# Four conditioning units of a hybrid layer moved from a feed-forward loop to the gaps between attention heads

## The chip, the cores and the metric

The kernel runs on one core of one Trainium2 chip. The metric is the device time of one execution in microseconds (us), as the median of several executions. A profile comes from one further execution, taken by the hardware profiler; its time is given beside the median below.

## What is computed

One layer of a streaming encoder for two requests that share the weights: 1024 prompt frames, and 32 frames of a running stream with caches and states. D is 1024. Cut to what matters here:

```python
mod = jax.nn.silu(c) @ w_ada + b_ada                       # c: one vector per request
sh1, sc1, g1, sh2, sc2, g2 = jnp.split(mod[:, None, :], 6, axis=-1)
h = x * (1 + sc1) + sh1
mq, mk, mv, mo, mi, mf, fq, fk, fv, ff, gu, gv = jnp.split(h @ w_in, split_at, axis=-1)
...                                                        # mLSTM (4 heads), FoX attention (8 heads), gMLP gate
mix = jnp.concatenate([hm, hf, hg], axis=-1) @ w_o
x = _layer_norm(ALPHA * x + (1 + g1) * mix, ln1_g, ln1_b)
h = x * (1 + sc2) + sh2
y = (jax.nn.silu(h @ w_gate) * (h @ w_up)) @ w_down
x = _layer_norm(ALPHA * x + (1 + g2) * y, ln2_g, ln2_b)
```

The first lines are adaLN: six vectors of 1024 values for each request, made from the conditioning vector c. The last of them, `g2`, is used only where the result of the feed-forward's down projection is added to the residual.

## The kernel before, in words

**Numbers and groups.** The 1056 frames stand on the free axis in two groups: group 0 has 512 columns, group 1 has 544. Every large product is done in float32r as three matmuls, with weights and operand each split in a high and a low part (`gemm`, L111 to L119: high by high L117, high by low L118, low by high L119). A weight block of 512 KB is loaded into the ring `raw` (3 buffers of pool `wp`), cast by ScalarE to `whi` (L105), and VectorE makes `wlo` (L106). All loads (L87) and stores (L91) that are spoken of here go through SyncE's queue (SP), one after another.

**The adaLN units.** `mod` is made in 24 units of 256 columns (`ada`, L171 to L189). A unit loads two halves of 512 KB of `w_ada`, does 16 matmuls of 32 x 256 (L179) into one PSUM bank, in four strips of the array, copies the result with ScalarE (L182, `adas`), transposes it with two matmuls into the other half of the same bank (L185), and VectorE reduces it (L187, `adam`) and writes the columns of `mod` (`ada_end`, L191). Units 0 to 7 (`sh1`, `sc1`) are done in the first product. Twelve units, 16 to 19 (`g1`) and 8 to 15 (`sh2`, `sc2`), are done in phase one by `more(n)` (L1344): their weights go to the two buffers `late` of pool `pl`, so a unit takes both, and their bank is one of the two of pool `pt` (tag `t`). Units 20 to 23 (`g2`) are done in the feed-forward of group 0.

**Phase one (up to about 360 us of the span).** A list written out by hand, `ORDER` (L42), says in which order the head projections (`q`, `k`), the first half of the FoX heads (`f`), the mLSTM chunks (`m`), the token-major projections (`v`, `o`) and single adaLN units (`a`) are emitted. PSUM has the ring `g` of three banks (pool `pg`) for the large products, two banks `t`, two `s`, and one `o`.

**Between the phases (to about 475 us).** The columns of the mixers' results for group 0 are read back from a DRAM tile `dmix` (`wo_mix`, loads named `mlstm_al`), group 0's residual is loaded (`wo_z<-xT`, eight loads, L978), the gMLP part runs (`evac_gv`, `evac_gmlp`, with ScalarE's copy `tm_gms`, L703, and its store to `dmix`), and the last projections of the heads' queries and keys (`fm_unit` with `evac_qk`, L359 to L367), then the output projection of group 0 and its layer norm (`ln1`, L1025 to L1042).

**Group 0's feed-forward (to about 886 us).** The rest of the mixers (`mixers`, L1272: second half of the FoX heads, five mLSTM chunks, the sample's attention `foxs`) is emitted first, then the loop over the groups of feed-forward columns (`GROUPS`, L33). `up` (L1072) makes gate and up products in the ring `g` (the program's name is `up_g`), reads them with ScalarE and VectorE (L1090 to L1096), and `down` accumulates groups of three or four columns into the residual. Inside the first columns stands the loop body with `if j < 4`: after each of columns 0 to 3, one adaLN unit 20 + j whose weights go to the ring `raw` and whose bank is one of the three of ring `g`.

At the sixth group (`g == WOB`) the mixers' pools are closed, and group 1's output projection (`wo(1)`) follows: its operand comes from `dmix` through `wo_tmp` loads into pool `pb`, with the casts L975 and L976 (`wo_mix`, L960), and its residual by eight `wo_z` loads. The rest is group 1's feed-forward and the two last layer norms.

**What sets the order.** The program is written in an order, but the Tile scheduler (`schedule_with_timeline_sim=True`) decides in which order each engine's instructions are issued. The order is fixed when the kernel is built; on the chip every engine works its list off in order and waits where an operand or a buffer isn't ready. So a change in one place can move rows elsewhere.

Of the kernel before, what the change touches and what calls it, by code (L numbers as in the profile page):

```python
# [38 lines left out]
MLB = (1, 2, 3, 4, 5)  # L39
RESE = "pp"  # L40
TAFF = ("aaaaaaaa", "aaaaaaav")
ORDER = "k0 k1p q0 f0 q1 a f1 s a q2 f2 a q3 f3 a v q4 f4 a q5 f5 o a m0 q6 f6 a m1 q7 m2 f7 a m3"  # L42
ADAPOS = 4
GENG = (0, 1, 1, 0)
FP = (0, 0)
RAW = 3
# [10 lines left out]
def weave(*parts):  # L57

    parts = list(parts)
    while parts:  # L60
        for p in list(parts):
            if next(p, parts) is parts:
                parts.remove(p)
# [6 lines left out]
class Kernel:  # L70
# [1215 lines left out]
    def run(self):  # L1286
# [52 lines left out]
        sl = ExitStack()  # L1339
        self.pl = self.pada = self.pool("pl", ctx=sl)  # L1340
        w1 = d["w_in_v"]
        rest = list(range(16, 20)) + list(range(8, 16))

        def more(n):  # L1344
            for u in rest[:n]:
# [34 lines left out]

        for x in ORDER.split():
            if x[0] in "fm" and HPA:
# [51 lines left out]
        for g, (j0, nj) in enumerate(GROUPS):  # L1434
            if g == WOB:
                s4.close()
                s3.close()
                self.pu, self.utag = self.pool("pu", 3, space=PSUM), "gu"
                pb = self.pb = self.pool("pb", side="right")
                weave(self.up(0, j0 + 1, act, pa, MM[0]))  # L1440
                self.operand(1, pb)
                with tc.issue_after(self.lastz.ins):
                    self.wo_mix(1, self.KORDER)
                stb = self.ln_begin(nc.gpsimd)
                self.wo(1, stb, MM[1], nc.vector, pb)
                self.operand(1, pb)

                def norm():
                    for a, b in MM[1]:
                        yield from self.ln1(1, stb, a, b)  # L1450

                self.sums()

                def fill():
                    for j in range(j0 + 2, j0 + nj):
                        self.sums()
                        yield from self.up(0, j, act, pa, MM[0])

                weave(fill(), norm())
                continue  # L1460
            for j in range(j0 + (g > 0), j0 + nj + (g < last)):
                weave(self.up(0, j, act, pa, WIDE if 0 < j < GROUPS[-1][0] else MM[0]))
                if j < 4:
                    self.ada(20 + j, self.wp, "raw", RAW, self.pg, "g")
            if g == WOB - 1:
                st = self.ln_begin(nc.gpsimd, sum=False)
                self.down(0, g, act, WIDE, st)
            else:
                self.down(0, g, act, WIDE)
# [160 lines left out]
```

## Time and profile before

| what | value |
|---|---|
| median of 3 runs | 1384.97 us (1381.76 to 1388.18) |
| profiled execution, its own time | 1386.62 us |
| its span | 1384.6 us |
| mean granted TensorE clock | 0.99 |
| TensorE (PE) busy | 1343.1 us, 97% |
| VectorE (DVE) busy | 1031.2 us, 74% |
| ScalarE (ACT) busy | 655.5 us, 47% |
| GpSimd (POOL) busy | 244.8 us, 18% |

The span is the time from the first to the last instruction that the profiler recorded; the profiled execution took 2 us more than that and lies 1.65 us above the median. "Granted clock" is the share of its full speed at which TensorE was clocked. Rows of the timeline give the start, the duration, the engine, the line and the tiles of an instruction, and in brackets how long its engine stood idle before it and whose end it waited for. A number such as x16 is a run of equal instructions; the duration is then that of the run. SPq is the queue in which SyncE issues DMAs: its durations are those of the issue, not of the transfer.

### The profile page before, as it was taken

To read this page: it belongs to the slowest core of one execution; us is meant where nothing else is said; L and a number is where in the kernel's file an instruction comes from. 1 tells how busy PE (TensorE), PEld (TensorE's weight loads), DVE (VectorE), ACT (ScalarE), POOL (GpSimd) and SP (SyncE) were. 2 spreads that over 40 slices of the span, in tenths; PEclk is the share of its full clock that TensorE was granted. 3 is DMA by queue.
4 is the path that set the end of the run, shared out by engine and by line. 5 is a ranking of instruction groups with operands and counts; after the bars stand their busy time and mean duration, and the time that the engine had idled before them with its cause. 6 is when DMAs were issued, how large, how long until landed. Compare 5 with 4: busy or idle time off the path is not lost.

```text
span 1384.6 us, 25402 instructions
## 1 busy us (share of the span) xinstructions
PE 1343.1 (97%) x9459; PEld 1226.1 (89%) x9459; DVE 1031.2 (74%) x2190; ACT 655.5 (47%) x1281; POOL 244.8 (18%) x276
## 2 busy tenths in 40 slices
PE   7999999999999899999999999999999999999996
PEld 4799788989899778888887889899999999999996
DVE  5547774678778757777776766678898988888777
ACT  3313354554545544545544455335564454545355
POOL 0102100042157500000000000264610000000341
PEclk9999999999999999999999999999999999999998
DMA  9763475455764765544444343564596768453321
GB/s 359 248 222 103 138 238 165 133 166 155 251 194 145 204 197 154 142 140 120 135 120 95 108 119 94 189 175 130 157 241 183 211 161 218 133 175 116 101 90 65
DMA packets 126386, 224.67 MB, mean 162 GB/s; under 512 B 21284, under 2 KB 70060, under 8 KB 126264
## 3 DMA queue, kind: packets, MB, share of 16 engines
q1 hardware_dynamic: 120952, 212.95, 49.4%
q0 software_dynamic: 5168, 9.96, 4.8%
q8 instruction: 75, 1.23, 0.4%
q14 instruction: 47, 0.39, 0.1%
q10 hardware_dynamic: 144, 0.14, 0.0%
HBM read 191.21 MB, written 51.72 MB: 175 GB/s over the span
## 4 chain that ended last, share of the span: by engine, by line
PE 83%; DVE 9%; DMA 4%; ACT 2%; issue 2%; POOL 1%; SPq 0%; DVEq 0%; ACTq 0%; POOLq 0%
PE up_g L117 5%; PE up_g L118 5%; PE up_g L119 5%; PE dn_g L119 4%; PE dn_g L117 4%; PE dn_g L118 4%; PE tm_g L282 3%; PE tm_g L283 3%; PE tm_g L284 3%; PE sup_u L119 3%; PE sup_u L117 3%; PE sup_u L118 3%; PE wo_g L118 2%; PE wo_g L119 2%; PE wo_g L117 2%; PE fox_t L788 2%
## 5 line engine op out<-in xcount | busy, mean ns | idle before, releaser
L117 PE MATMUL up_g<-mlstm_ah,up_whi 128*128 128x512 f32 (+1 forms) x384 | 141.3, 368 | 4.2 <-ACT lna_tmp L1037 3.4
L118 PE MATMUL up_g<-mlstm_al,up_whi 128*128 128x512 f32 (+1 forms) x384 | 141.5, 369 | 0.6 <-DVE mlstm_al L1042 0.6
L119 PE MATMUL up_g<-mlstm_ah,up_wlo 128*128 128x512 f32 (+1 forms) x384 | 140.7, 367 | 0.0
L283 PE MATMUL tm_g<-tm_wlo,start_h1h 128*128 128x256 f32 (+1 forms) x384 | 109.8, 287 | 0.0
L282 PE MATMUL tm_g<-tm_whi,start_h1h 128*128 128x256 f32 (+1 forms) x384 | 109.3, 287 | 0.0
L284 PE MATMUL tm_g<-tm_whi,start_h1l 128*128 128x256 f32 (+1 forms) x384 | 108.8, 285 | 0.0
L1161 ACT CAST sup_whi<-sup_raw 128x1024 fp32r<-128x1024 f32 x54 | 56.0, 1047 | 90.8 <-PE dn_u L118 47.4
L117 PEld LDWEIGHTS up_g<-mlstm_ah,up_whi 128*128 128x128 f32 x384 | 73.2, 191 | 16.9 <-ACT mlstm_ah L1041 3.6
L761 ACT ACTIVATE fox_p<-fox_s,fox_fmx 128x384 f32<-128x384 f32 (+2 forms) x96 | 55.2, 578 | 60.6 <-DVE fox_fmx L759 44.3
L118 PEld LDWEIGHTS up_g<-mlstm_al,up_whi 128*128 128x128 f32 x384 | 73.1, 190 | 11.9 <-DVE mlstm_al L1042 1.2
L119 PEld LDWEIGHTS up_g<-mlstm_ah,up_wlo 128*128 128x128 f32 x384 | 73.2, 191 | 10.6
L105 ACT CAST up_whi<-up_raw 128x1024 fp32r<-128x1024 f32 x50 | 52.4, 1048 | 61.6 <-PE up_g L118 18.2
L106 DVE TENSOR_TENSOR up_wlo<-up_raw,up_whi 128x1024 fp32r<-128x1024 f32 x50 | 66.8, 1336 | 14.0 <-ACT up_whi L105 13.3
L1016 DVE SCALAR_TENSOR_TENSOR wo_z<-dn_g,start_mod,wo_z 128x512 f32<-128x512 f32 (+4 forms) x120 | 60.2, 520 | 21.5 <-PE dn_g L119 19.6
L1162 DVE TENSOR_TENSOR sup_wlo<-sup_raw,sup_whi 128x1024 fp32r<-128x1024 f32 x54 | 68.1, 1264 | 10.5 <-ACT sup_whi L1161 10.5
L283 PEld LDWEIGHTS tm_g<-tm_wlo,start_h1h 128*128 128x128 f32 x384 | 72.3, 188 | 2.3 <-issue 2.1
L282 PEld LDWEIGHTS tm_g<-tm_whi,start_h1h 128*128 128x128 f32 x384 | 72.1, 189 | 1.7 <-issue 0.8
L117 PE MATMUL dn_g<-up_acth,dn_whi 128*128 128x512 f32 (+2 forms) x200 | 73.5, 368 | 0.0
L118 PE MATMUL dn_g<-up_actl,dn_whi 128*128 128x512 f32 (+2 forms) x200 | 73.4, 368 | 0.0
L119 PE MATMUL dn_g<-up_acth,dn_wlo 128*128 128x512 f32 (+2 forms) x200 | 73.3, 366 | 0.0
L284 PEld LDWEIGHTS tm_g<-tm_whi,start_h1l 128*128 128x128 f32 x384 | 72.2, 188 | 0.1
L117 PE MATMUL fm_g<-start_h1h,fm_whi 128*128 128x272 f32 (+2 forms) x200 | 60.6, 312 | 5.9 <-DVE fm_qkl L367 2.0
(628 smaller groups left out, 4628.9 us busy)
## 6 DMA issues: line engine op xcount, KB each, us to landing
up_raw<-w_gu SPq DMA_DIRECT2D x50, 512.0 KB
dn_raw<-w_dn SPq DMA_DIRECT2D x28, 512.0 KB
ada_late<-w_ada SPq DMA_DIRECT2D x24, 512.0 KB
wo_raw<-w_o SPq DMA_DIRECT2D x24, 512.0 KB
sup_raw<-w_gu SPq DMA_DIRECT2D x20, 512.0 KB
start_dp<-w_gu SPq DMA_DIRECT2D x19, 512.0 KB
start_dp<-w_gu POOLq DMA_DIRECT2D x19, 512.0 KB, 7.8
sup_raw<-start_dp SPq DMA_DIRECT2D x18, 512.0 KB
```

Source lines behind the costliest of these rows:

```text
L105: nc.scalar.copy(hi[:, :w], raw[:, :w])
L106: (eng or nc.vector).tensor_tensor(lo[:, :w], raw[:, :w], f(hi[:, :w]), ALU.subtract)
L117: nc.tensor.matmul(ps, hi, xh(k), start=start and k == 0, stop=False)
L118: nc.tensor.matmul(ps, hi, xl(k), start=False, stop=False)
L119: nc.tensor.matmul(ps, lo, xh(k), start=False, stop=stop and k == n - 1)
L282: nc.tensor.matmul(ps[:, :ncol], xh, hi, start=k == 0, stop=False)
L283: nc.tensor.matmul(ps[:, :ncol], xh, lo, start=False, stop=False)
L284: nc.tensor.matmul(ps[:, :ncol], xl, hi, start=False, stop=k == 7)
L761: nc.scalar.activation(pr[:, lo:hi], banks[x][:, :hi - lo], AF.Exp, bias=mxs[:, 0:1], accum_out=sums[:, x:x + 1])
L1016: self.lastz = self.nc.vector.scalar_tensor_tensor(z[:, m, x:y], ps[:, x - a:y - a], g[i], z[:, m, x:y], ALU.mult, ALU.add)
L1161: nc.scalar.copy(h, x)
L1162: tt(l, x, f(h), ALU.subtract)
```

## The change

Units 20 to 23 are appended to the list of the units of phase one, `ORDER` gets four more `a`, and the two lines in group 0's feed-forward loop are gone. So these units use the buffers `late` and a bank `t` instead of `raw` and a bank `g`. The number of instructions of every engine and their shapes stay the same.

```diff
-ORDER = "k0 k1p q0 f0 q1 a f1 s a q2 f2 a q3 f3 a v q4 f4 a q5 f5 o a m0 q6 f6 a m1 q7 m2 f7 a m3"
+ORDER = "k0 k1p q0 f0 q1 a f1 s a q2 f2 a q3 f3 a v a q4 f4 a q5 f5 a o a m0 q6 f6 a m1 a q7 m2 f7 a a m3"
...
-        rest = list(range(16, 20)) + list(range(8, 16))
+        rest = list(range(16, 20)) + list(range(8, 16)) + list(range(20, 24))
...
             for j in range(j0 + (g > 0), j0 + nj + (g < last)):
                 weave(self.up(0, j, act, pa, WIDE if 0 < j < GROUPS[-1][0] else MM[0]))
-                if j < 4:
-                    self.ada(20 + j, self.wp, "raw", RAW, self.pg, "g")
```

The scheduler's order differs at three places of interest.

First, SP's queue at the end of phase one. `wo_raw`, `dvn` and `traw` are weights and tiles of the gMLP part, `dmix_32` and `dmix_33` the mixers' results of groups 0 and 1, `mlstm_al` the operand of group 0's output projection, `wo_z` its residual. Before:

```order
L87 DMA wo_raw_4952<-w_o 128x1024
L91 DMA start_dvn_63<-tm_traw_4548 128x256
L87 DMA wo_raw_4989<-w_o 128x1024
L91 DMA start_dvn_63<-tm_traw_4585 32x256
L91 DMA o_vn<-tm_traw_4585 32x256
L87 DMA tm_gvn_4726<-start_dvn_63 128x512
L91 DMA start_dmix_32_88<-fox_fo_3904 64x512
L91 DMA start_dmix_32_88<-mlstm_mixs_4006 128x2x128
L87 DMA mlstm_al_4021<-start_dmix_32_88 128x512 x6
L87 DMA wo_z_787_4040<-xT 128x512 x8
L91 DMA start_dmix_33_89<-tm_gms_4670 128x2x256
```

The same stretch of the changed kernel:

```order
L91 DMA start_dvn_63<-tm_traw_4636 128x256
L87 DMA ada_late_3996<-w_ada 128x1024
L87 DMA ada_late_4002<-w_ada 128x1024
L91 DMA start_dvn_63<-tm_traw_4673 32x256
L91 DMA o_vn<-tm_traw_4673 32x256
L87 DMA tm_gvn_4814<-start_dvn_63 128x512
L91 DMA start_dmix_32_88<-fox_fo_3969 64x512
L91 DMA start_dmix_33_89<-tm_gms_4758 128x2x256
L91 DMA start_dmix_32_88<-mlstm_mixs_4094 128x2x128
L87 DMA tm_gvn_4854<-start_dvn_63 32x256
L87 DMA mlstm_al_4109<-start_dmix_32_88 128x512 x6
L87 DMA wo_z_807_4128<-xT 128x512 x8
```

The two loads of the last adaLN unit stand in the queue here, and the store of `tm_gms` for group 1, which stood behind the eight `wo_z` loads, now stands ahead of them and of the `mlstm_al` loads.

Second, TensorE's list at the start of group 0's feed-forward, where the first column's last gate and up matmuls stand (`up_g` with three different numbers: three banks of ring `g`). Before:

```order
L119 MATMUL up_g_8087<-mlstm_ah_4020,up_wlo_8001 128x256
L117 MATMUL up_g_8062<-mlstm_ah_4020,up_whi_7994 128x256
L117 MATMUL up_g_8087<-mlstm_ah_4020,up_whi_8000 128x256
L179 MATMUL ada_g_8119<-ada_raw_8120,start_c_63_182 32x256 x4
L179 MATMUL ada_g_8119<-ada_raw_8126,start_c_63_182 32x256 x4
L118 MATMUL up_g_8062<-mlstm_al_4021,up_whi_7994 128x256
```

The changed kernel at the same place:

```order
L119 MATMUL up_g_8175<-mlstm_ah_4108,up_wlo_8089 128x256
L117 MATMUL up_g_8150<-mlstm_ah_4108,up_whi_8082 128x256
L117 MATMUL up_g_8175<-mlstm_ah_4108,up_whi_8088 128x256
L117 MATMUL up_g_8221<-mlstm_ah_4108,up_whi_8211 128x512
L118 MATMUL up_g_8221<-mlstm_al_4109,up_whi_8211 128x512
L119 MATMUL up_g_8221<-mlstm_ah_4108,up_wlo_8212 128x512
```

Where the adaLN unit took the next bank of ring `g`, the second column's gate product takes it now.

Third, TensorE's list at the end of group 0's feed-forward: `fox_o` is the output of the last FoX head, `dn_g` a block of 128 rows of the down projection (eight blocks of 12 matmuls in this group, here the third), `dn_t` the sum for the layer norm's pivot. Before:

```order
L801 MATMUL fox_o_7931<-fox_pth_7975,fox_v_7806 128x256
L796 MATMUL fox_o_7931<-fox_ptl_7976,fox_v_7806 64x256
L801 MATMUL fox_o_7931<-fox_pth_7975,fox_v_7806 128x256
L894 MATMUL dn_t_10079<-wo_z_787_4040,start_ones_45_140 128x512
L118 MATMUL dn_g_10104<-up_actl_9856,dn_whi_10100 128x512
L119 MATMUL dn_g_10104<-up_acth_9855,dn_wlo_10101 128x512
```

The changed kernel, at the end of the last of the eight blocks (`dn_g_10191`):

```order
L796 MATMUL fox_o_8019<-fox_ptl_8064,fox_v_7894 64x256
L801 MATMUL fox_o_8019<-fox_pth_8063,fox_v_7894 128x256
L894 MATMUL dn_t_10079<-wo_z_807_4128,start_ones_45_140 128x512
L118 MATMUL dn_g_10191<-up_actl_9712,dn_whi_10172 128x512
L119 MATMUL dn_g_10191<-up_acth_9711,dn_wlo_10173 128x512
L117 MATMUL dn_g_10191<-up_acth_9783,dn_whi_10172 128x512
L118 MATMUL dn_g_10191<-up_actl_9784,dn_whi_10172 128x512
```

Before, 62 matmuls of `dn_g` stood between the last FoX head and the `up` products that lead to group 1's output projection; now there are 8. The 96 `up` matmuls (128x256) behind them are the same in both.

## The prediction

> **What bounds the kernel now.** I read the page first: the busy times of the engines and the chain of waits.
>
> ```profile
> PE 1343.1 (97%) x9459; PEld 1226.1 (89%) x9459; DVE 1031.2 (74%) x2190; ACT 655.5 (47%) x1281; POOL 244.8 (18%) x276
> PE 83%; DVE 9%; DMA 4%; ACT 2%; issue 2%; POOL 1%; SPq 0%; DVEq 0%; ACTq 0%; POOLq 0%
> ```
>
> TensorE bounds the kernel: 97% of 1384.6 us, and 83% of the chain that ended last. It idles for 41.5 us in all. A change that leaves TensorE's work as it is can win only part of those, or of the time at a lower clock, and can lose by adding to either. The busy times by stretch show where they lie (columns: PE, PEld, DVE, ACT, POOL, then granted clock, DMA share, GB/s).
>
> ```profile
> 110.00:180.00 70.00, 66.66 (x452) 59.83 (x451) 52.28 (x144) 25.61 (x60) 12.25 (x22) 0.95 0.45 137
> 250.00:320.00 70.00, 67.13 (x512) 60.47 (x511) 49.39 (x140) 32.63 (x77) 15.22 (x16) 1.00 0.55 169
> 365.00:420.00 55.00, 53.02 (x424) 52.24 (x423) 40.24 (x56) 26.87 (x42) 25.65 (x26) 0.97 0.73 226
> 440.00:475.00 35.00, 28.84 (x221) 27.23 (x220) 28.85 (x62) 21.10 (x49) 26.60 (x33) 0.95 0.54 152
> 475.00:540.00 65.00, 64.67 (x402) 50.48 (x401) 38.48 (x97) 31.78 (x71) 0.74 (x1) 0.97 0.70 199
> 540.00:900.00 360.00, 357.86 (x1908) 301.93 (x1907) 261.92 (x537) 172.91 (x345) 15.53 (x19) 1.00 0.44 126
> ```
>
> Phase one has idle time, 3.34 us in 110 to 180 and 2.87 us in 250 to 320. Group 0's feed-forward, which the units leave, has nearly none: 0.33 us in 475 to 540 and 2.14 us in the 360 us behind. So there is no gap that the units' going closes, and what decides is how the waits at three or four places move.
>
> **The change part by part.**
>
> *A. The moved work.* The timeline shows one unit at each place, its 16 matmuls and its two transposes with the row behind them.
>
> ```profile
> 256.47 1.07 PE L179 MATMUL ada_t<-ada_late,start_c 128*32 128x256 f32 x16
> 261.35 0.38 PE L185 MATMUL ada_t<-start_ident,ada_adas 128*128 128x128 f32 x2
> 261.49 0.36 PE L284 MATMUL tm_g<-tm_whi,start_h1l 128*128 128x256 f32 x1
> ...
> 491.16 1.07 PE L179 MATMUL ada_g<-ada_raw,start_c 128*32 128x256 f32 x16
> 492.16 0.50 PE L117 MATMUL up_g<-mlstm_ah,up_whi 128*128 128x512 f32 x1
> 492.50 0.40 PE L118 MATMUL up_g<-mlstm_al,up_whi 128*128 128x512 f32 x1
> 492.73 0.40 PE L119 MATMUL up_g<-mlstm_ah,up_wlo 128*128 128x512 f32 x1
> ```
>
> The matmuls take 1.07 us in both places; the next row starts 1.00 us after them and 0.14 us after the transposes. With 0.1 us for each of two changes of tile (the row behind takes 0.50 instead of the 0.40 of the two behind it) a unit costs 1.35 us of TensorE. Four leave the feed-forward (-5.4) and four enter phase one (+5.4): 0. The eight loads of 512 KB change queue places but not number.
>
> *B. The banks of the feed-forward.* The tiles `ada_g` borrowed a bank of ring `g` between the gate and up products. Two rows show a wait at such a place.
>
> ```profile
> 473.55 1.07 PE L179 MATMUL ada_g<-ada_raw,start_c 128*32 128x256 f32 x16 [1.69 <-DVE up_sil L1093]
> 478.41 0.50 PE L117 MATMUL up_g<-mlstm_ah,up_whi 128*128 128x512 f32 x1 [0.34 <-DVE ada_adam L187]
> ```
>
> The second wait, for the reduction of the unit, goes: -0.34. The first is a wait for a bank that VectorE was still reading (`up_sil`). In the changed order the second column's gate product (`up_g_8221`) stands where the unit stood and needs the same bank, so the wait stays; only if VectorE has read the bank sooner does it go as well. Bounds -2.0 (0.34 and 1.69) and 0; I take -0.3, since the bank's reader is unchanged.
>
> *C. The clock in the feed-forward.* Three stretches of a few us around the third unit:
>
> ```profile
> 502.00:506.00 4.00, 4.00 (x33) 3.26 (x32) 2.53 (x5) 1.69 (x3) 0.00 (x0) 1.00 0.11 44
> 508.00:511.50 3.50, 3.50 (x36) 2.40 (x35) 1.54 (x4) 1.52 (x5) 0.00 (x0) 1.00 0.63 195
> 511.50:515.00 3.50, 3.50 (x15) 1.94 (x15) 2.42 (x3) 1.37 (x4) 0.00 (x0) 0.53 0.84 232
> ```
>
> TensorE has no idle time in any of them, yet from 511.5 to 515 the granted clock is 0.53, behind a stretch of 32-row adaLN matmuls and small matmuls of the sample's attention. At 0.53 the 3.5 us do what 1.9 us would do: 1.6 us lost. The stretch from 502 to 506, with the sample's matmuls but without a unit, kept 1.00. With the units gone the drop may go (-1.6) or not (0). I take -1.2, three quarters of it, since the row with small matmuls alone kept its clock.
>
> [...]
>
> *D. The transition from phase one.* Here stands the wait that the changed SP order touches.
>
> ```profile
> 362.64 5.97 SPq L87 DMA_DIRECT2D wo_z<-xT  x8
> 369.34 0.38 SPq L91 DMA_DIRECT2D start_dmix<-tm_gms  x1
> ...
> 374.91 0.59 ACT L703 COPY tm_gms<-tm_g 128x512 f32<-128x512 f32 x1 [4.96 <-DMA start_dmix<-tm_gms]
> ...
> 371.39 0.39 PE L117 MATMUL fm_g<-start_h1h,fm_whi 128*128 128x272 f32 x1 [1.98 <-DVE fm_qkl L367]
> ...
> 372.00:374.00 2.00, 2.00 (x10) 2.00 (x10) 0.00 (x0) 0.00 (x0) 0.18 (x1) 0.50 1.06 373
> 374.00:376.00 2.00, 2.00 (x13) 1.97 (x12) 0.00 (x0) 1.09 (x2) 0.00 (x0) 0.71 0.98 317
> ```
>
> The store of `tm_gms` stands in SP's queue behind eight residual loads, and its data moves while the DMA engines are full (share 1.06). ScalarE waits 4.96 us for that store, since its tile has one buffer, and the `g` banks that it reads are held: TensorE waits 1.98 us, and then runs at 0.50 and 0.71 for 4 us, which costs 1.0 and 0.6 us. Together 3.6 us. In the changed order the store stands ahead of the eight loads. But the queue then carries two adaLN loads just ahead, and an instruction that waits there holds the whole queue. Bounds: -3.6 (all gone) and +2 (another wait of 1.98 us in its place). I take -2, a little over half of the gain, since the store is moved but the eight loads still fill the engines right behind it.
>
> *E. New loads in phase one.* Twelve units stand there now.
>
> ```profile
> L179 PE MATMUL ada_t<-ada_late,start_c x192: 379/379/636, 66.2 to 355.6; 128*32 128x256 f32 x192
>   DMA ada_late<-w_ada: 2.8, 1
> ...
> 156.63 0.83 SPq L87 DMA_DIRECT2D ada_late<-w_ada  x2
> 160.97 1.08 PE L179 MATMUL ada_t<-ada_late,start_c 128*32 128x256 f32 x8 [2.81 <-DMA ada_late<-w_ada]
> ...
> 160.00:165.00 5.00, 4.03 (x21) 3.25 (x22) 2.27 (x8) 3.12 (x9) 0.54 (x1) 0.51 0.88 294
> ```
>
> One unit of twelve waited for its loads: issued at 156.63, used at 160.97, 4.3 us later, with 2.81 us of idle time and then a clock of 0.51 for some 4 us (2 us more). A unit occupies both `late` buffers, so its loads can't be issued before the last unit's matmuls, and a second unit close behind the first (the `a a` after `f7`) has to bridge those 4.3 us with other work; in the changed list 34 rows of TensorE stand between. As often as before, four units give 4/12 of 2.81: +0.9. Bounds 0 (each load hidden like eleven of twelve) and +4.8 (one such wait with its clock).
>
> *F. The last FoX head and group 1's output projection.* The mixers' chain of waits isn't shortened by the change, but it starts 5.4 us later and the feed-forward beside it has 5.4 us less to do; in the changed order the last head ends in the last down block.
>
> ```profile
> 870.82 1.02 PE L894 MATMUL dn_t<-wo_z,start_ones 128*128 128x512 f32 x2
> 871.87 0.45 SPq L91 DMA_DIRECT2D start_dmix<-fox_fo  x1
> 874.16 0.33 SPq L87 DMA_DIRECT2D wo_tmp<-start_dmix  x1
> 874.58 3.23 SPq L87 DMA_DIRECT2D wo_z<-xT  x7
> ...
> 887.44 2.73 SPq L87 DMA_DIRECT2D wo_tmp<-start_dmix  x4
> 897.70 0.29 PE L117 MATMUL wo_g<-up_ah,wo_whi 128*128 128x272 f32 x1
> 897.83 0.29 PE L118 MATMUL wo_g<-up_al,wo_whi 128*128 128x272 f32 x1
> 901.15 0.43 DVE L976 TENSOR_TENSOR up_al<-wo_tmp,up_ah 128x272 fp32r<-128x272 f32 x1
> ```
>
> From the head's end at 870.82 to the output projection at 897.70 lie 26.9 us. Now 54 fewer `dn_g` matmuls stand there (62 before, 8 after), each of 512 columns like the rows under A, which follow one another every 0.23 us (492.50 to 492.73): 12.4 us, so about 14.5 us are left. The chain needs 3.3 us to the first load (870.82 to 874.16) and, once the loads flow, 14.1 us to the last cast (887.44 to 901.58): 17.4. TensorE asks for the last operand only at the end of the first block row of `wo_g`, 48 matmuls of 0.13 us (897.70 to 897.83) or 6.2 us after its start: 20.7. A slack of 3.3 us, then. But the eight `wo_z` loads, 8 x 278 KB = 2.2 MB or 6.0 us at 373 GB/s, seven of which were issued from 874.58 on and had the time to themselves, now fall between the operands. Bounds: 0, and +5 (6.0 less 3.3 is 2.7 of idle time, and about 2 of lower clock as in D and E). I take +1.5, nearer to 0, as the changed order puts only four of the loads ahead of most of the operands.
>
> *Sum.* 0 - 0.3 - 1.2 - 2.0 + 0.9 + 1.5 = -1.1 us against the profiled execution's 1386.62: 1385.5. The median of the runs is 1.65 us lower than that execution, so on that scale 1383.9, in round numbers **1384.0**. Half a per cent, about what a measurement of this kernel can tell from no change, is 6.9 us: below 1378.0 and above 1391.9.
>
> **The rivals.**
>
> *Faster: the freed ring.* Here the units' place in the ring was what cost: B goes whole (-2.0), C whole (-1.6), D whole (-3.6), E and F are hidden. That is -7.2 against 1384.97: 1377.8. For it speaks that each of these waits stands in a row above; against it that B's wait has an unchanged reader, and that three things must go right at once, with nothing late next.
>
> *Slower: the mixers' chain becomes the bound ahead of `wo(1)`.* TensorE has no more work to put beside the last head, and waits for store, load and cast. It decides as soon as the operand loads are delayed by more than the slack of 3.3 us. The eight residual loads (6.0 us) and three `w_o` blocks of 512 KB (4.2 us at 373 GB/s) in front of all operands would make 10.2 - 3.3 = 6.9 us idle, and 2 us of lower clock: +8.9; with B, C and E as forecast (-0.6), and D at 0, +8.3 against 1384.97: 1393.3. For it: the 62 matmuls have become 8, and a program whose filler shrinks while its chain does not must wait somewhere. Against it: not all loads stand in front, and 54 matmuls of `dn_g` are cover that the last head now had for itself.
>
> *No effect because nothing moves.* The rows of the order show the units in their new place and TensorE's list changed, so this has no chance worth a number; a total of zero by cancelling is my forecast's own case.
>
> **How the numbers follow.** The forecast gets 0.62: with any one term at either of its ends and the others as taken, the sum lies between -2.8 (B) and +2.9 (D), far within half a per cent. The freed ring gets 0.16, as it needs all of B to D; the chain ahead of `wo(1)` 0.22, as one cause alone decides it and E may add to it. For the range I take 1376.0 (the freed ring, and most of phase one's one wait of 2.81 us gone as well) to 1394.0 (the chain's case); outside is left about one in ten on each side. The chances of faster and slower by over 0.5% are those of the rivals, which end just beyond the bounds: 0.15 and 0.22, with 0.63 within.
>
> **What would show each step right or wrong.** A: the L179 rows of tile `ada_late` become x256, and the time from 475 to 870 falls by 5.4 us while phase one grows by as much. B: no wait for `ada_adam`, and still one of 1 to 2 us for `up_sil` at the first column's end. C: a clock of 1.00 through the sample's attention. D: the store of `tm_gms` lands before the `wo_z` loads are issued, ScalarE's wait of 4.96 us is gone, and the clock from the transition on is 1.00. E: the waits for `ada_late` stay at one, or come at the two units behind the last head. F: between the last `fox_o` and the first `wo_g`, no idle time and a full clock. The prediction is wrong if TensorE's idle time ahead of `wo(1)` exceeds 5 us, if a queue held by an adaLN load delays weights of phase one by more than 5 us, or if the stretches without any such wait differ by more than 1 us from before, for which I have no cause.

## The result, and the profile after

The changed kernel takes 1397.06 us (median of 5 runs, 1392.75 to 1398.19), the kernel before 1386.75 us (5 runs). The ratio is 1.007 with a 95% interval of 1.0055 to 1.0086: slower by about 10 us, outside the forecast's range. The profiled execution took 1397.91 us, with a span of 1395.9 us against 1384.6.

The page of the changed kernel, busy times and chain of waits:

```profile
PE 1344.2 (96%) x9459; PEld 1226.7 (88%) x9459; DVE 1034.1 (74%) x2190; ACT 656.2 (47%) x1281; POOL 249.7 (18%) x276
PE 77%; DVE 10%; DMA 7%; ACT 2%; issue 2%; POOL 1%; SPq 1%; DVEq 0%; ACTq 0%; POOLq 0%
```

TensorE is busy for as long as before (1344.2 against 1343.1 us). Nearly all of the added time is idle time: 51.7 us now, 41.5 before. In the chain, DMA has risen from 4% to 7%. Where the time lies is seen by the same landmarks in both traces:

| landmark on TensorE | before | after | difference so far |
|---|---|---|---|
| first matmul behind the layer norm's wait (`up_g`, wait for `lna_tmp`) | 466.16 | 471.18 | +5.0 |
| first matmul of group 1's output projection (`wo_g`) | 897.70 | 905.37 | +7.7 |
| the wait for `up_wlo` behind it | 1010.31 | 1021.28 | +11.0 |
| end of the span | 1384.6 | 1395.9 | +11.3 |

The first 5.0 us are in the main the four units' own work, now ahead of the first landmark (0.86 us of it is the layer norm's wait, 4.24 us where it was 3.38). Behind it the units' 5.4 us should have been won back. Instead another 2.7 us were lost up to `wo_g` (so 8 us of new loss there), and 3.3 us at its start. The busy times by stretch of the changed kernel:

```profile
365.00:420.00 55.00, 52.58 (x432) 51.47 (x431) 40.34 (x62) 27.38 (x44) 23.41 (x22) 1.00 0.76 240
475.00:540.00 65.00, 56.16 (x311) 45.71 (x311) 35.42 (x76) 27.40 (x62) 3.55 (x8) 0.92 0.50 130
...
485.00:495.00 10.00, 2.88 (x13) 2.09 (x12) 6.61 (x12) 7.39 (x13) 0.73 (x1) 0.88 0.41 118
495.00:505.00 10.00, 10.00 (x62) 7.59 (x62) 2.96 (x6) 1.99 (x3) 0.00 (x0) 0.78 0.29 89
```

From 475 to 540 TensorE was busy for 64.67 us before; now it is 56.16, at a clock of 0.92. Between 485 and 495 it works for 2.88 us of 10. The waits are in the timeline of TensorE:

```profile
478.56 0.50 PE L117 MATMUL up_g<-mlstm_ah,up_whi 128*128 128x512 f32 x1 [1.72 <-DVE up_sil L1093]
...
494.57 0.80 PE L117 MATMUL up_g<-mlstm_ah,up_whi 128*128 128x512 f32 x1 [7.12 <-DVE up_sil L1092]
495.17 0.63 PE L118 MATMUL up_g<-mlstm_al,up_whi 128*128 128x512 f32 x1
...
910.84 0.52 PE L117 MATMUL wo_g<-up_ah,wo_whi 128*128 128x272 f32 x2 [2.30 <-ACT up_ah L975]
```

The first wait, 1.72 us, is the one that the forecast expected to stay (1.69 before). The second, 7.12 us, is new: the up product of the second column needs a bank of ring `g`, and VectorE has not read the first column's gate product (L1092). Behind it the granted clock is 0.50 from 494.57 to 499.46, which costs 2.4 us more (a matmul takes 0.63 instead of 0.40 us). The third, 2.30 us, is new too.

Why the bank was read so late is seen on the engines that read it. ScalarE and then VectorE of the changed kernel:

```profile
486.12 0.42 ACT L576 ACTIVATE mlstm_mo<-mlstm_mo 128x256 f32<-128x256 f32 x1 [7.18 <-DMA mlstm_mo<-start_dmo]
...
487.92 0.38 ACT L1089 ACTIVATE up_sil<-up_g 128x256 f32<-128x256 f32 x1
...
489.85 0.63 ACT L587 ACTIVATE mlstm_mw<-mlstm_mw 128x512 f32<-128x512 f32 x1 [0.32 <-DVE mlstm_mw L585]
...
492.21 0.41 ACT L1091 ACTIVATE up_sil<-up_sil 128x256 f32<-128x256 f32 x1
```

```profile
488.20 1.62 DVE L585 SCALAR_TENSOR_TENSOR mlstm_mw<-mlstm_mb,start_col,start_maskbig 128x128 f32<-128x128 f32 x4 [3.68 <-DMA mlstm_mb<-start_dM]
...
490.11 1.23 DVE L106 TENSOR_TENSOR up_wlo<-up_raw,up_whi 128x1024 fp32r<-128x1024 f32 x1
...
491.70 2.36 DVE L106 TENSOR_TENSOR up_wlo<-up_raw,up_whi 128x1024 fp32r<-128x1024 f32 x2
494.10 0.42 DVE L1092 TENSOR_TENSOR up_sil<-up_g,up_sil 128x256 f32<-128x256 f32 x1
```

ScalarE waits 7.18 us for a load of the first mLSTM chunk (`mlstm_mo`), and the first exponential of the gate product (L1089) stands behind that wait. VectorE waits 3.68 us for another load of the chunk (`mlstm_mb`); behind it come four mLSTM instructions and three weight splits (L106), and only then the read of the bank. The same rows of the kernel before, ScalarE, then VectorE and the first matmul of the second column's up product on TensorE:

```profile
478.37 0.38 ACT L1089 ACTIVATE up_sil<-up_g 128x256 f32<-128x256 f32 x1
481.39 0.42 ACT L576 ACTIVATE mlstm_mo<-mlstm_mo 128x256 f32<-128x256 f32 x1 [2.64 <-DMA mlstm_mo<-start_dmo]
```

```profile
482.21 1.14 DVE L585 SCALAR_TENSOR_TENSOR mlstm_mw<-mlstm_mb,start_col,start_maskbig 128x128 f32<-128x128 f32 x4 [2.25 <-DMA mlstm_mb<-start_dM]
483.27 0.41 DVE L1092 TENSOR_TENSOR up_sil<-up_g,up_sil 128x256 f32<-128x256 f32 x1
...
484.12 0.40 PE L117 MATMUL up_g<-mlstm_ah,up_whi 128*128 128x512 f32 x1
```

There the first exponential came ahead of the wait, and the read right behind the mLSTM instructions, with no split between. The read stood behind the two loads before, too; it ended at 483.68, and TensorE came to the up product at 484.12. So it was in time by 0.4 us. In the changed kernel TensorE is done with the gate product at 487.46, and the read ends at 494.52.

The order that does this stands in the lists. ScalarE's list of the changed kernel, where `up_sil_8142` is the first column and `up_g_8150` its gate bank:

```order
L1094 COPY up_acth_8078<-up_sil_8142 128x256
L576 ACTIVATE mlstm_mo_6413<-mlstm_mo_6413 128x256
L577 ACTIVATE mlstm_mo_6413<-mlstm_mo_6413,start_ones_36_112 128x256
L105 COPY up_whi_8217<-up_raw_8215 128x1024
L1089 ACTIVATE up_sil_8142<-up_g_8150 128x256
```

Before, the unit's copy and the exponential stood ahead of L576:

```order
L1094 COPY up_acth_7990<-up_sil_8054 128x256
L182 COPY ada_adas_8132<-ada_g_8119 128x256
L105 COPY up_whi_8151<-up_raw_8149 128x1024
L1089 ACTIVATE up_sil_8054<-up_g_8062 128x256
L576 ACTIVATE mlstm_mo_6325<-mlstm_mo_6325 128x256
```

On TensorE, 13 matmuls of the second column's gate product had taken the place of the unit (the first three are shown with the change); they put off the end of the first column's gate product, and with it its readers, behind the mLSTM chunk.

### The profile page after: what moved, and what is told of

It reads as the page before. It is cut to its first block, busy times and chain, and to the rows that moved or that the text cites. A ratio compares the mean times of both kernels' runs of the same rounds, so it can differ in the third digit from the quotient of the medians.

```text
span 1395.9 us, 25402 instructions
## 1 busy us (share of the span) xinstructions
PE 1344.2 (96%) x9459; PEld 1226.7 (88%) x9459; DVE 1034.1 (74%) x2190; ACT 656.2 (47%) x1281; POOL 249.7 (18%) x276
## 4 chain that ended last, share of the span: by engine, by line
PE 77%; DVE 10%; DMA 7%; ACT 2%; issue 2%; POOL 1%; SPq 1%; DVEq 0%; ACTq 0%; POOLq 0%
PE up_g L117 5%; PE up_g L118 5%; PE up_g L119 5%; PE dn_g L117 4%; PE dn_g L119 4%; PE dn_g L118 4%; PE tm_g L282 3%; PE tm_g L283 3%; PE tm_g L284 3%; PE sup_u L119 2%; PE sup_u L118 2%; PE sup_u L117 2%; PE fox_t L788 2%; PE sup_g L119 2%; PE sup_g L118 2%; PE wo_g L118 2%
## 5 line engine op out<-in xcount | busy, mean ns | idle before, releaser
L106 DVE TENSOR_TENSOR up_wlo<-up_raw,up_whi 128x1024 fp32r<-128x1024 f32 x50 | 63.0, 1261 | 11.7 <-ACT up_whi L105 11.3
L793 ACT CAST fox_pth<-fox_t 128x512 fp32r<-128x512 f32 (+1 forms) x80 | 40.8, 545 | 65.1 <-PE fox_t L788 65.0
```

The costliest lines, as they stand in the source:

```text
L106: (eng or nc.vector).tensor_tensor(lo[:, :w], raw[:, :w], f(hi[:, :w]), ALU.subtract)
```

## The experiments

Theory P (order): the loss comes from the reads of the first column's banks, which in the changed order stand behind instructions that wait for the mLSTM chunk's loads. Rival Q: phase one pays for the four added units. Rival R: the loss lies at the start of group 1's output projection, where too little work stands beside the last FoX head. Each row below has its own comparison with the kernel before on the same chip (medians 1385.68 to 1387.27 us). A profile is one execution and not the median: that of one_stays took 1379.17 us, that of mlstm_late 1390.61, that of before_late 1393.25. So the profiles are read for single waits and the order of rows, and the times for the totals.

| kernel | median us | ratio to before | 95% interval |
|---|---|---|---|
| one_stays | 1384.25 | 0.9986 | 0.9974 to 0.9997 |
| none | 1388.27 | 1.0018 | 1.0007 to 1.0028 |
| both | 1389.79 | 1.0026 | 1.0009 to 1.0042 |
| mlstm_late | 1383.92 | 0.9988 | 0.9973 to 1.0003 |
| mo_late | 1396.76 | 1.0059 | 1.0037 to 1.0081 |
| mb_late | 1390.28 | 1.0019 | 1.0001 to 1.0037 |
| lo_late | 1394.72 | 1.0056 | 1.0037 to 1.0075 |
| col1_after | 1395.85 | 1.0064 | 1.0042 to 1.0086 |
| one_pt | 1489.76 | 1.0733 | 1.0714 to 1.0752 |
| before_late | 1384.63 | 0.9987 | 0.9973 to 1.0001 |
| one_late | 1386.41 | 0.9996 | 0.9980 to 1.0012 |
| z_late | 1396.49 | 1.0071 | 1.0050 to 1.0091 |

**Which part of the change costs: one_stays, none, both.** The first puts one of the four units back:

```diff
-        rest = list(range(16, 20)) + list(range(8, 16)) + list(range(20, 24))
+        rest = list(range(16, 20)) + list(range(8, 16)) + list(range(21, 24))
...
                 weave(self.up(0, j, act, pa, WIDE if 0 < j < GROUPS[-1][0] else MM[0]))
+                if j == 0:
+                    self.ada(20, self.wp, "raw", RAW, self.pg, "g")
```

and takes one `a` out of `ORDER` (the one behind `v a`). 

> One unit (20) goes back into group 0's first feed-forward column, three stay moved. Theory P (order): the 7.1 us wait at the second column's up product comes from the list order, in which the reads of the gate bank stand behind the first mLSTM chunk's loads on ScalarE and VectorE; with one unit back the reads of the first column stand ahead again, so the wait and its half clock (about 9.5 us together) go: 1387 to 1389 us. Rival Q (phase one pays for the added units) and rival R (too little work beside the last FoX head ahead of group 1's output projection) both expect three quarters of the loss to stay: about 1394.5 us.

Measured: 1384.25 us, 12.8 us below the changed kernel's median, for one unit of four. Its timeline has the wait for the unit's reduction again and no long one, as the row of the stretch behind it shows:

```profile
476.24 0.50 PE L117 MATMUL up_g<-mlstm_ah,up_whi 128*128 128x512 f32 x1 [0.34 <-DVE ada_adam L187]
...
475.00:540.00 65.00, 64.67 (x367) 52.98 (x366) 43.71 (x95) 32.51 (x69) 0.74 (x1) 1.00 0.58 159
```

The three units that stay moved cost nothing: Q and R expected most of the loss to stay.

The kernel none is the kernel before without the two lines of the loop and with `mod` set to zero. 

> Units 20 to 23 are done nowhere (the multipliers of g2 are left at zero, so the gate of the feed-forward's result is left out), which takes 5.4 us of TensorE away; phase one is as before the change, the feed-forward as after it. P: the lists of ScalarE and VectorE have the order of the changed kernel, so the wait is there although no unit was added anywhere: 1386.75 - 5.4 + 9.5 = about 1391 us. Q: phase one pays nothing, so about 1381.4. R: only the wait ahead of group 1's output projection (2.3 us) stays: about 1384.

Measured: 1388.27 us, though 5.4 us of work are gone. TensorE's wait is there with nothing added in phase one:

```profile
488.46 0.79 PE L117 MATMUL up_g<-mlstm_ah,up_whi 128*128 128x512 f32 x1 [6.54 <-DVE up_sil L1093]
```

So it is the taking away of the units from the feed-forward, not their coming into phase one. Between the first two landmarks this kernel takes 434.1 us (465.67 to 899.81), the changed kernel 434.2 and the kernel before 431.5. The time is 2.7 us better than P said (1391).

The kernel both is the changed kernel with the loop's two lines kept. 

> Units 20 to 23 are done twice, in phase one as in the changed kernel and again in group 0's feed-forward as before. P: only their 5.4 us of TensorE are added to before, and no long wait in the feed-forward: about 1392 us. Q: the whole loss and the work besides: about 1402. R: filler as before, so also about 1392.

Measured: 1389.79 us, 3.3 us above before for four units of more work, and no wait in the first columns but the 0.34 us for the reduction and 0.93 us for the bank. Q's 1402 falls with this.

**The proof by the order alone: mlstm_late.** All four units stay moved; instructions of the mLSTM chunk are queued behind reads of the first column, by edges that set the order of issue and wait for nothing:

```diff
         x = nc.scalar.activation(mo[:L], mo[:L], AF.Exp, scale=-1.0)
+        if j == 4:
+            self.early = [x]
...
             x = nc.vector.scalar_tensor_tensor(w[:L, h, :L], mb[:L, h, :L], col[:L, 0, h:h + 1],
                                                self.maskbig[:L, :L], ALU.subtract, ALU.max)
+            if j == 4:
+                self.early.append(x)
...
+                if j == 0:
+                    for i, e in zip(self.early, (self.lastexp, self.lastmul, self.lastmul, self.lastmul, self.lastmul)):
+                        tc.add_manual_dep(i.ins, e.ins.name, NOSYNC, reason="issue_after")
```

`lastexp` is the last exponential of the first column on ScalarE, `lastmul` its last multiplication on VectorE. 

> The changed kernel, all four units moved, with one thing more: on ScalarE and VectorE the first instructions of the first mLSTM chunk behind group 0 are queued behind the first feed-forward column's reads of its banks. P: the wait of 7.1 us shrinks to under 1.5 us and its half clock goes: 1387 to 1390 us. Q and R: nothing changes, about 1397.

Measured: 1383.92 us. Its timeline (lines are one to five higher here): TensorE's waits, then ScalarE's rows.

```profile
478.80 0.50 PE L118 MATMUL up_g<-mlstm_ah,up_whi 128*128 128x512 f32 x1 [1.00 <-DVE up_sil L1098]
488.39 0.50 PE L118 MATMUL up_g<-mlstm_ah,up_whi 128*128 128x512 f32 x1 [0.68 <-DVE up_sil L1097]
...
485.31 0.38 ACT L1094 ACTIVATE up_sil<-up_g 128x256 f32<-128x256 f32 x1
...
487.06 0.42 ACT L1096 ACTIVATE up_sil<-up_sil 128x256 f32<-128x256 f32 x1
487.38 0.40 ACT L577 ACTIVATE mlstm_mo<-mlstm_mo 128x256 f32<-128x256 f32 x1
```

The wait of 7.12 us has become one of 0.68, with every unit where the change put it, and up to some 500 us TensorE's matmuls stand in the same order in both traces. So the order of the reads makes this wait: for it P is shown, and Q is not the cause. The whole loss is gone (1383.92 against 1397.06), but more than five instructions stand elsewhere: from some 500 us on the scheduler ordered the lists anew, 38 `dn_g` matmuls stand behind the last FoX head in place of 8, and the wait at `wo_g` is gone as well. R's place is thus a part of the loss and not its main cause.

The times of these four kernels all lie 2 to 6 us below what P said. In one_stays and mlstm_late the wait at `wo_g`, which P had left out, goes too and makes up a good part of it; for none and both the difference stays unexplained.

**Which of the waits in the way sets the price: mo_late, mb_late, lo_late.** The first has only ScalarE's edge, the second only VectorE's four.

> The changed kernel, with ScalarE's first instruction of the mLSTM chunk (the one that waits for the load of mlstm_mo) queued behind the first column's reads; VectorE keeps its order. If ScalarE's wait for mlstm_mo sets the price, the 7.1 us wait goes and the time is 1385 to 1388. If VectorE's wait for mlstm_mb and the three weight splits behind it set it, the banks come free hardly sooner (from the changed kernel's rows: the wait for mlstm_mb ends at 488.2, its four instructions at 489.8, three splits of 1.2 us each at 493.5), the wait is still 6 to 7 us and the time about 1396.

> The changed kernel, with only VectorE's four instructions on mlstm_mb queued behind the first column's reads; ScalarE keeps its wait for mlstm_mo in front. If mlstm_mo on ScalarE alone sets the price, nothing changes: about 1397. If mlstm_mb on VectorE alone sets it, the wait goes: 1385 to 1388. By the rows of the changed kernel both stand in line, ScalarE's wait ends at 486.1 and the last exponential could come at about 490.5, so the bank is read at about 491.5 in place of 494.5: a wait of about 4 us, and about 1392 us.

In the third, VectorE's work of the third column is queued behind `lastmul` instead (the loop body for j == 2 inside `tc.issue_after(self.lastmul.ins)`). 

> The changed kernel, with VectorE's work of the third feed-forward column (two weight splits of 1.2 us) queued behind the first column's reads; both waits for the mLSTM loads stay in front. By the rows, ScalarE's last exponential ended at 492.6 and the read could begin there in place of 494.1: the wait falls from 7.1 to about 5.5 us, time about 1395. If the splits were the cause it would go, 1387.

Measured: 1396.76, 1390.28 and 1394.72 us. The waits of TensorE at this place, one row from each kernel (for mb_late also the read of the bank, L1097 there, and the first matmul of the up product):

```profile
492.46 0.79 PE L118 MATMUL up_g<-mlstm_ah,up_whi 128*128 128x512 f32 x1 [6.08 <-DVE up_sil L1095]
```

```profile
486.34 1.11 PE L858 MATMUL foxs_s<-foxs_k,foxs_q 66*32 66x256 f32 x8 [3.13 <-DMA foxs_k<-start_dsf]
...
487.97 0.42 DVE L1097 TENSOR_TENSOR up_sil<-up_g,up_sil 128x256 f32<-128x256 f32 x1
488.45 0.80 PE L118 MATMUL up_g<-mlstm_ah,up_whi 128*128 128x512 f32 x1
```

```profile
490.95 0.79 PE L117 MATMUL up_g<-mlstm_ah,up_whi 128*128 128x512 f32 x1 [3.63 <-DVE up_sil L1092]
```

No single piece sets the price. Without ScalarE's wait for `mlstm_mo` in front, 6.08 us remain, as forecast from VectorE's rows (6 to 7). In mb_late another wait shows, 3.13 us for the load of `foxs_k`, since TensorE's list has the sample's attention behind the gate product there. But the bank came free only at 488.39: TensorE had ended the gate product at 483.22, so 5.2 us of lateness are hidden behind the sample's attention, where I had forecast about 4 from the rows of both engines. In lo_late the wait fell by 3.5 us (7.12 to 3.63), more than the 1.6 that I had worked out for the splits; but the load of `mlstm_mb` took 4.3 us there (480.84 to 485.17) and 5.8 in the changed kernel, so a part of it is the load's. Only both edges together, in mlstm_late, take the wait away.

**The place on TensorE: col1_after.** The second column's matmuls are queued behind the first's last one (`with tc.issue_after(self.lastmm.ins)` around the loop body for j == 1). 

> The changed kernel, with TensorE's work of the second column queued behind the last matmul of the first, as the unit had kept it apart before; nothing else is touched. If the 13 gate matmuls of the second column that took the unit's place are what put ScalarE's read behind the mLSTM chunk's wait, the read stands ahead of it again and the time is 1385 to 1389. If the order on ScalarE and VectorE comes from elsewhere, it stays at about 1397.

Measured: 1395.85 us, although ScalarE's first exponential now stands ahead of L576. SP's rows, then the read of the bank and TensorE's wait:

```profile
482.44 0.29 SPq L91 DMA_DIRECT2D start_dsf<-foxs_p  x1
487.02 0.69 SPq L87 DMA_DIRECT2D foxs_qp<-start_dsf  x1
...
489.14 0.42 DVE L1092 TENSOR_TENSOR up_sil<-up_g,up_sil 128x256 f32<-128x256 f32 x1
...
490.60 1.11 PE L853 MATMUL foxs_s<-foxs_k,foxs_q 66*32 66x256 f32 x8 [4.30 <-DMA foxs_k<-start_dsf]
```

My expectation was wrong in two ways. The first exponential is only one of the steps: VectorE's read still stands behind its wait for `mlstm_mb` and a split, and the bank comes free at 489.56, 3.2 us behind the end of the gate product (486.31). And the next thing in TensorE's line here is the sample's attention, which waits until 490.60: it stores a small tile to DRAM and reads it back, and the read is issued 4.6 us after the store. The wait at `wo_g` stays too (2.50 for 2.30 us). What the shorter wait saves (4.30 for 7.12 us) is lost to the clock: it is 0.50 from 759.2 to 762.5 and from 909.4 to 912.7 (a matmul of `wo_g` takes 0.43 us there, 0.29 ahead of it), where the changed kernel has 1.00.

**The unit's bank: one_pt.** As one_stays, but the unit's bank comes from the two banks `t`:

```diff
-                    self.ada(20, self.wp, "raw", RAW, self.pg, "g")
+                    self.ada(20, self.wp, "raw", RAW, self.pt, "t")
```

> Unit 20 stays in group 0's first feed-forward column as in one_stays, but in a bank t in place of a bank of ring g. If what helped there is the 1.35 us of other work for TensorE, the wait for the second column's bank is gone here too and the time is near one_stays, 1384 to 1386. If it is the turn in ring g, which puts the first column's reads ahead of the mLSTM chunk on ScalarE, the wait is there again: ScalarE's wait for mlstm_mo stands in front in this order, VectorE has only one weight split ahead of the read in place of three, so 3 to 4 us of wait and its clock, about 1390.

Measured: 1489.76 us, far from both. Two stretches of all engines, then the unit and the next down product on TensorE, show why:

```profile
540.00:650.00 110.00, 91.73 (x460) 74.34 (x460) 76.16 (x190) 50.71 (x116) 3.25 (x7) 0.92 0.41 116
650.00:800.00 150.00, 109.78 (x509) 87.92 (x509) 95.87 (x248) 57.73 (x140) 2.17 (x5) 0.76 0.36 96
...
767.89 1.07 PE L179 MATMUL ada_t<-ada_raw,start_c 128*32 128x256 f32 x16
771.84 0.50 PE L117 MATMUL dn_g<-up_acth,dn_whi 128*128 128x512 f32 x1 [1.95 <-DVE wo_z L1016]
```

The turns at the banks `t` went by the order in which the program asks for them, and all mixers, which use these banks, are written ahead of the feed-forward: the unit came at 767.9, behind the mixers' last `fox_t` (766.05). VectorE needs the unit's columns to read the first two blocks of the first down group: the other six were read by 556, these two only from 771.0 on, and by the program they held two of the three banks of ring `g` until then. From 619.5 to 771.8 TensorE has no matmul of the feed-forward, and the mixers ran alone. From 540 to 800 it has 201.5 us of work in 260, and a clock down to 0.76. For the question asked, the local wait was 3.39 us for `up_sil` at 488.28 (expected 3 to 4 for the turn in the ring), but the run as a whole does not decide it, as the lists differ everywhere behind.

**Do the repairs help by themselves: before_late, one_late.** The first has the edges of mlstm_late in the kernel before, the second both repairs.

> The kernel before, with the same queueing as in mlstm_late. In its profile TensorE does not wait for the first column's reads, so if that queueing helps only by taking away the wait that the change made, nothing is gained here: 1385 to 1388. If it helps by itself, by 2 us or more: 1382 to 1384.

> One unit stays (as in one_stays) and the mLSTM chunk is queued as in mlstm_late. If both take away the same wait, they don't add up: 1383 to 1385, as each alone. If they take away different things: 1381 to 1382.

Measured: 1384.63 and 1386.41 us, both with 1 inside the interval (0.4 us below the 1385 to 1388 and 1.4 us above the 1383 to 1385 that I had given). So the edges gain nothing that shows where no bank hangs on them, and the repairs don't add up. one_stays is the only version whose interval lies below 1, by 0.03 to 0.26%: none of these beats the kernel before by an amount worth the name.

**The second wait: z_late.** The changed kernel with group 1's residual loads queued behind operand loads (`with self.tc.issue_after(self.half.ins)` around the load of `wo_z`). 

> The changed kernel, with the first four residual loads of group 1 behind four operand loads in SP's queue, and the others behind the last operand load of the first column half. If the residual loads among the operands make the 2.3 us wait at the start of group 1's output projection, it falls to under 1 us and the time to 1394 or 1395. If the late end of the last FoX head and the four operand buffers alone make it, the wait stays at 2 us or more and the time at 1396 to 1397. The 7.1 us wait in the feed-forward is untouched by either.

Measured: 1396.49 us, and 1.78 us of wait at `wo_g` in place of 2.30. That is between the two expectations, nearer to the second; it doesn't settle what makes this wait. What the other runs say: of all kernels but one_pt, those with 8 `dn_g` matmuls behind the last FoX head all have the wait (after 2.30, mo_late 2.67, lo_late 1.81, col1_after 2.50, z_late 1.78 us); with 62 (before, both, before_late) and 38 (one_stays, none, mlstm_late, mb_late, one_late) it is absent. The last head ends at 885 us or later in the first five, and at 881 or earlier in the others. A late last head goes with the wait. That the operand ring of four buffers lengthens it is only argued from one row, in which ScalarE waits for a load in the midst of the casts and SP's four loads took 4.68 us to issue (2.73 us before, at 887.44):

```profile
898.40 4.68 SPq L87 DMA_DIRECT2D wo_tmp<-start_dmix  x4
...
910.37 1.61 ACT L975 CAST up_ah<-wo_tmp 128x272 fp32r<-128x272 f32 x4 [1.40 <-DMA wo_tmp<-start_dmix]
```

## Why the prediction was wrong, step by step

- **A was right in the main.** The first landmark came 5.0 us later for 5.4 us of moved work; 0.86 us of it is the layer norm's longer wait, so the units took somewhat less than that. none, whose phase one has no unit more, reaches it at 465.67 (466.16 before).
- **B failed, and with it the prediction.** It took the reader of the bank to be unchanged ("the wait stays", -0.3, bounds -2.0 and 0). The 1.69 us wait did stay (1.72), the 0.34 went. But the next use of the ring, one bank later, waits 7.12 us, and the half clock after it costs 2.4 us: about +9.5 where B had -0.3. The readers had changed: not what they do, but where they stand in the lists of ScalarE and VectorE. I had read TensorE's and SP's lists and not those of the two engines that free the banks, where the exponential had moved behind L576 and three splits ahead of L1092. The bound of 0 on the bad side had no row behind it. A load of 4.3 us stood in E's rows; one such load in front of a reader would have given a bound of some +4 here. Of the signs that the prediction named for being wrong, the last came: the stretch from 475 to 540, which has neither of the two waits named ahead of it, has 8.5 us less of TensorE's work. The rival of the freed ring was wrong the other way round: the unit's turn in the ring was what held the order.
- **C had the wrong cause.** The unit was made to answer for the half clock at 511.5 to 515. The changed kernel has the same without any unit near it (last section), and both, with all four units there, keeps 1.00 from 485 to 540. So the -1.2 was not the units' to give: 0 came of it.
- **D gave less than forecast.** From 365 to 420 the clock went from 0.97 to 1.00, 1.65 us in 55, and the idle time from 1.98 to 2.42; the 1.98 us wait became three of 0.87, 0.98 and 0.57 us. That is -1.2 for the forecast -2. But ScalarE's wait for a store of `tm_gms` only moved to the next copy, as the store ahead of that copy still stands behind the eight residual loads in SP's queue (it is issued at 378.98):

```profile
385.96 0.21 ACT L703 COPY tm_gms<-tm_g 128x64 f32<-128x64 f32 x1 [5.70 <-DMA start_dmix<-tm_gms]
```

  From 362 us to the first landmark TensorE's idle time rose from 5.89 to 7.64 us, which takes the gain back. And that the store caused the 1.98 us was argued: the row names VectorE's read of `fm_qkl`.
- **E was too dear.** There is one load wait of 2.89 us (2.81 before) and none was added: 0 for +0.9. A stretch at half clock is new in phase one, from 322.0 to 325.3 (some 1.7 us), behind a wait of 1.81 us for `mlstm_mqk`; no run shows whether the units' loads put it there.
- **F was right in kind and too small.** The operand waits 2.30 us, and by the landmarks 3.3 us are lost there, for +1.5 within bounds of 0 and +5. TensorE came to `wo_g` 14.5 us behind the last head (890.9 to 905.4), exactly as worked out, so the row count was a good instrument. The rival that had the kernel slower through this chain alone (+8.3) gave the sign, but not the main cause: its place holds a third of the loss (3.3 of 11.3 us).

## What to carry to other kernels

When an instruction that uses a ring of banks or buffers is moved, read the new order of the engines that free the ring, not only of the one that waits for it: a release that slips behind an instruction waiting for a DMA comes as late as that DMA and all the work queued between (here 7.1 us). A small piece of work with its turn in a ring can hold an order together that was good by luck (here by 0.4 us); if it has to go, pin the releases ahead of whatever waits for memory (five edges were worth 13 us here). And where a release takes steps on two engines, clear the way on both: one edge alone left it 6.1 or 5.2 us late (mo_late, mb_late).

## What the runs showed of the hardware that I had not expected

In the changed kernel the clock fell to half without idle time ahead of it and without an adaLN unit near. Its timeline, and the stretch:

```profile
525.00 0.42 PE L878 MATMUL foxs_o<-foxs_pth,foxs_v 128*64 128x32 f32 x4
...
526.15 0.39 PE L117 MATMUL up_g<-mlstm_ah,up_whi 128*128 128x512 f32 x1
...
527.12 0.63 PE L119 MATMUL up_g<-mlstm_ah,up_wlo 128*128 128x512 f32 x1
...
526.00:530.00 4.00, 4.00 (x13) 3.24 (x12) 2.10 (x7) 1.42 (x5) 0.00 (x0) 0.60 0.51 139
```

From 526.77 to 530.10 the clock was 0.50, and matmuls of 512 columns took 0.63 us (0.39 ahead of it and behind it). A stretch of the sample's output matmuls with 32 columns each lies just ahead; TensorE was busy for all of the 27.31 us before (499.46 to 526.77), at a clock of 1.00. What makes the clock fall there is not shown. It does not always come: from 500 to 540 the profiles of one_stays, none and both kept 1.00, while before had 0.83 from 505 to 515 and mo_late 0.83 from 515 to 525, both with TensorE busy throughout from 495 on, and mlstm_late 0.83 from 505 to 515, behind 1.66 us of idle time between 495 and 505. So a term for it belongs into the range and not into the sum.

These small loads took long: the load of `mlstm_mo` (128 x 256 values) was issued at 481.13 and used at 486.12, 5.0 us later, and that of `mlstm_mb` 5.8 us after its issue (482.39 to 488.20); before, it was 4.8 us (476.62 to 481.39) and 4.4 us (477.85 to 482.21). SP's queue in the changed kernel shows the load of `mlstm_mb` with the next chunk's load behind it, which waits for the buffer (5.4 us of it for the load that is still coming in) and holds the queue (7.82 us for the two; the next issue is at 491.37):

```profile
481.13 0.34 SPq L87 DMA_DIRECT2D mlstm_mo<-start_dmo  x1
482.39 7.82 SPq L87 DMA_DIRECT2D mlstm_mb<-start_dM  x2
491.37 0.35 SPq L87 DMA_DIRECT2D up_raw<-w_gu  x1
```
